# The state's output and the Toeplitz loads issued by GpSimd, an eighth buffer for sample keys and values

## The chip, the cores and the metric

The kernel runs on one core of a Trainium2 chip. The metric is the device time of one execution in microseconds (us). The core's engines run at the same time, each through its own instructions in a fixed order, and wait for each other by semaphores: TensorE (PE in the profile; PEld is its weight load), VectorE (DVE), ScalarE (ACT), GpSimd (POOL) and SyncE (SP), which here does nothing but issue transfers (DMAs). ScalarE issues DMAs too. A DMA that waits for something holds up all that stands behind it in the queue of its issuer.

## What is computed

One inference step of a hybrid decoder layer for a prompt of 1024 tokens and a sample group of 8 x 4 tokens with cached state, all with shared weights. The part that the change touches is the first mixer: attention heads beside a diagonal state-space model (S5), both fed from one projection.

```python
def trunk_layer(x, h0_re, h0_im, mem_k, mem_v, attend, w_in, ...):
    proj = x @ w_in
    q, k, v, u = jnp.split(proj, [D_ATT, 2 * D_ATT, 3 * D_ATT], axis=-1)
    o_att = attend(q, k, v).reshape(Bn, L, D_ATT)
    y_ssm, h_re, h_im = s5_mixer(u, h0_re, h0_im, a_re, a_im, log_dt, b_re, b_im, c_re, c_im, d_skip, w_glu, b_glu)
    mixed = jnp.concatenate([rms_norm(o_att, g_att), rms_norm(y_ssm, g_ssm)], axis=-1) @ w_out
    x = layer_norm(DEEPNORM_ALPHA * x + mixed, ln1_g, ln1_b)
    x = layer_norm(DEEPNORM_ALPHA * x + memory_attention(x, mem_k, mem_v, w_mem_q, w_mem_o), ln2_g, ln2_b)
    ffn = (jax.nn.silu(x @ w_gate) * (x @ w_up)) @ w_down
    return layer_norm(DEEPNORM_ALPHA * x + ffn, ln3_g, ln3_b), k, v, h_re, h_im
```

`s5_mixer` runs, for 32 groups of 16 channels, a complex state of 64 through a scan over the positions, `h_t = A h_(t-1) + B u_t`, with `y_t = Re(C h_t) + D u_t`, then GELU and a gate; it returns the last state as well. For the sample tokens, `attend` reads 1024 cached keys and values.

## The kernel before

Matrix products are made of three float32r products each (high part by high part, high by low, low by high), so a line like L209 to L211 is one step of a product. The run goes through: projection (u, q, k, v) with the state-space model and the sample attention woven in, up to about 345 us; prompt attention, gate and output; memory attention; feed-forward. The change lies in the first of these.

*The state-space model* (`ssm`, L1338 on) runs in two halves (`qf`), 16 of the 32 groups each, stored as 8 pairs of groups. Tokens are cut into chunks of 8. In a half, Bs and CA are built on VectorE and GpSimd (L1426 to L1428), TensorE transposes Bs into ET (L1437) and computes the taps kp (L1448), which go to DRAM as s_kp (L1454). TensorE then makes the chunk inputs from ET and U (L1466), ScalarE puts them into HX (L1468). HX is 128 partitions by 8 pairs by 2 (real, imaginary) by 145 columns. The tile M (named ET in the trace, because it takes over ET's buffer) is the Toeplitz matrix of the taps, read back from s_kp by 8 DMAs (L1471); it needs all L1466 to be over. VectorE then scans HX (`step`, L1479 to L1483): first inside blocks of 8 chunks, then 15 steps over the blocks, the last of which writes column 136. Then HX is corrected (L1495 to L1500), the real part on VectorE and the imaginary on GpSimd, in two blocks of four pairs. TensorE makes the outputs from M and U (L1510) and from CA and HX (L1514), ScalarE applies GELU into Y (L1517, named Bs), which goes out by 8 DMAs (L1522). The state's output (L1519) stores columns 136 to 144 of HX, 9 floats per pair and part.

*The sample attention* (`sample_attn`, `sample_finish`) takes keys (ckT) and values (cv) in chunks of four tiles of 128 x 512, all from one ring of buffers named skv, seven of them; five chunks for each of two groups of sequences. L712 makes the scores from a key tile and the queries qb, which GpSimd lays out (L726) from qs, written by ScalarE in four parts; L772 multiplies a value tile by the probabilities; L778 ends a group; VectorE reads its result in L780.

The order on each engine is set when the program is built, by a scheduler that places all instructions by their dependences; SP's queue holds the skv loads, the DMAs of the state-space model and, later, others.

Of the kernel before, what the change touches and what calls it, by code (L numbers as in the profile page):

```python
# [13 lines left out]
OP = mybir.AluOpType  # L14
# [126 lines left out]
class Body:  # L141
# [145 lines left out]
    def project(self, A, xa, og):  # L287
# [34 lines left out]
        with tc.tile_pool(name="ps_a", bufs=1, space=PSUM) as self.pp2, tc.tile_pool(name="ssm_small", bufs=1) as self.sp, tc.tile_pool(name="ssm_part", bufs=1) as sh, \  # L322
# [47 lines left out]

            ssm = self.ssm()
            next(ssm)

            def between(work, *at):
                for i, _ in enumerate(work):
                    for n, gen in at:
                        if i in n:
                            next(gen, None)

            between(self.gemm(4, 4, xa, evac_q), ((0, 4), ssm))  # L380
            sample = self.sample_attn(sap)
            between(self.gemm(8, 4, xa, evac_k), (range(1, 11), sample), ((5, 10), ssm))
            finish = self.sample_finish(*next(sample))
            between(self.gemm_v(12, 2, lhs_x, [8], evac_v, False), ((0,), finish), ((1,), ssm))
# [311 lines left out]
    def sample_attn(self, ap):  # L696
        nc, a = self.nc, self.a
        v, act, g, mm = nc.vector, nc.scalar, nc.gpsimd, nc.tensor.matmul
        mask, tsel, bsel = (self.t(ap, [128, n], f"sm{n}") for n in (704, 16, 8))
        for d, s in ((mask, a["mask_s"]), (tsel, a["toksel"]), (bsel, a["bsel"])):  # L700
            nc.sync.dma_start(d[:], s)

        def load(src, gr, c):
            t_ = [self.t(ap, [128, 512], "skv", bufs=7) for _ in range(4)]
            for b4 in range(4):
                nc.sync.dma_start(t_[b4][:], a[src][4 * gr + b4, c])
            return t_

        def scores(o, n, q, keys):
            for hp in range(4):  # L710
                for b4 in range(4):
                    mm(o[32 * b4:32 * b4 + 32, :n], q[:, hp, b4].rearrange("p h t -> p (h t)"), keys(b4, hp),  # L712
                       start=hp == 0, stop=hp == 3)

        def masked(gr, j, o, n, s0, m0):
            S, nm = probs[gr][:2]
            v.tensor_tensor_reduce(out=S[:, s0:s0 + n], in0=o, in1=mask[:, m0:m0 + n], scale=-1.0, scalar=3e38,
                                   op0=OP.add, op1=OP.min, accum_out=nm[:, j:j + 1])

        probs = []  # L720
        for gr in range(2):
            qb = self.t(ap, [128, 4, 4, 8, 4], "qb", bufs=2)
            g.memset(qb[:], 0.0)
            for hp in range(4):
                for z in range(2):
                    g.tensor_copy(out=qb[64 * z:64 * z + 64, hp, :, 2 * hp + z, :],  # L726
                                  in_=self.qs[64 * z:64 * z + 64, hp, 16 * gr:16 * gr + 16].rearrange("p (b t) -> p b t", t=4))
            probs.append((self.t(ap, [128, 672], "sS", bufs=2), self.t(ap, [128, 3], "snm", bufs=2), qb))
            for c in range(5):
                if c % 4 == 0:  # L730
                    ps = self.psq()
                kt = load("ckT", gr, c)
                scores(ps[:, 128 * (c % 4):], 128, qb, lambda b4, hp: kt[b4][:, 128 * hp:128 * hp + 128])
                if c >= 3:
                    w = 512 if c == 3 else 128
                    masked(gr, c - 3, ps[:, :w], w, 512 * (c - 3), 512 * (c - 3))
                yield
        yield ap, probs, load, scores, masked, tsel, bsel

    def sample_finish(self, ap, probs, load, scores, masked, tsel, bsel):  # L740
        nc, a = self.nc, self.a
        v, act, g, mm = nc.vector, nc.scalar, nc.gpsimd, nc.tensor.matmul
# [13 lines left out]
        for gr, (S, nm, qb) in enumerate(probs):  # L756
# [12 lines left out]
            for c in range(5):  # L769
# [2 lines left out]
                    mm(po[32 * b4:32 * b4 + 32, :], PT[:, 128 * c + 32 * b4:128 * c + 32 * b4 + 32], vt[b4][:],  # L772
                       start=c == 0, stop=False)
                yield
            vs = self.t(ap, [128, 512], "skv", bufs=7)
            nc.sync.dma_start(vs[:32], self.s_v[1024:1056, :])
            for b4 in range(4):
                mm(po[32 * b4:32 * b4 + 32, :], PT[:32, 640 + 32 * b4:672 + 32 * b4], vs[:32], start=False, stop=True)  # L778
# [556 lines left out]
    def ssm(self):  # L1335
        nc, a, sp, sh = self.nc, self.a, self.sp, self.sh
        H_ = lambda tag, shape: self.t(sh, list(shape), tag)
        v, g, act, mm = nc.vector, nc.gpsimd, nc.scalar, nc.tensor.matmul  # L1338
# [69 lines left out]
        H = lambda tag, shape: self.t(sh, list(shape), tag)  # L1408
        for qf in range(2):
            gs = slice(8 * qf, 8 * qf + 8)  # L1410

            Bs, CA = H("Bs", (128, 8, 2, 8, 16)), H("CA", (128, 8, 2, 9, 16))
            for i in range(4):
                l2, g2 = slice(2 * i, 2 * i + 2), slice(8 * qf + 2 * i, 8 * qf + 2 * i + 2)
                d1, d2, p1, p2 = (H(n_, (128, 2, 9, 16)) for n_ in ("d1", "d2", "p1", "p2"))
# [42 lines left out]
            HX = H("HX", (128, 8, 2, 145))  # L1458
# [9 lines left out]
                act.copy(HX[:, gl, :, 9:145], ps[:, 0:272].rearrange("p (r c) -> p r c", r=2))  # L1468
            M = H("ET", (128, 16, 128))
            for i in range(8):  # L1470
                nc.sync.dma_start(M[16 * i:16 * i + 16], self.s_kp[qf, :, :, 16 * i:16 * i + 128])  # L1471
            X = HX[:, :, :, 9:137].rearrange("p g r (J j) -> p g r J j", j=8)
            qa = lambda e_: e_[:, gs].unsqueeze(2)
            m1, m2 = S("w1", (128, 8, 2, 16)), S("w2", (128, 8, 2, 16))
# [1 line left out]
            def step(dst, src, are, aim, naim, w):  # L1476

                b1 = are.unsqueeze(2).unsqueeze(3).to_broadcast([128, 8, 2, w])
                tt(out=m1[:, :, :, :w], in0=src, in1=b1, op=OP.mult)  # L1479
                tt(out=m2[:, :, 0, :w], in0=src[:, :, 1], in1=naim.unsqueeze(2).to_broadcast([128, 8, w]), op=OP.mult)  # L1480
                tt(out=m2[:, :, 1, :w], in0=src[:, :, 0], in1=aim.unsqueeze(2).to_broadcast([128, 8, w]), op=OP.mult)
                tt(out=dst, in0=dst, in1=m1[:, :, :, :w], op=OP.add)
                tt(out=dst, in0=dst, in1=m2[:, :, :, :w], op=OP.add)  # L1483
# [3 lines left out]
                step(X[:, :, :, :, j], X[:, :, :, :, j - 1], QW[:, 0, 0, gs], QW[:, 0, 1, gs], nq[:, 0, gs], 16)  # L1487
            for J in range(1, 16):
                step(X[:, :, :, J, 7:8], X[:, :, :, J - 1, 7:8], QW[:, 7, 0, gs], QW[:, 7, 1, gs], nq[:, 7, gs], 1)
            for hh in range(2):  # L1490
                l4, g4 = slice(4 * hh, 4 * hh + 4), slice(8 * qf + 4 * hh, 8 * qf + 4 * hh + 4)
                for ri, e in ((0, v), (1, g)):
                    w_ = [H(n_, (128, 4, 15, 7)) for n_ in (("d1", "d2"), ("p1", "p2"))[ri]]
                    for sri, q_ in ((0, QW[:, 0:7, ri]), (1, nq[:, 0:7] if ri == 0 else QW[:, 0:7, 0])):
                        e.tensor_tensor(out=w_[sri][:], in0=X[:, l4, sri, 0:15, 7:8].to_broadcast([128, 4, 15, 7]),  # L1495
                                        in1=q_[:, :, g4].rearrange("p n g -> p g n").unsqueeze(2)
                                        .to_broadcast([128, 4, 15, 7]), op=OP.mult)
                    d_ = X[:, l4, ri, 1:16, 0:7]
                    e.tensor_tensor(out=d_, in0=d_, in1=w_[0][:], op=OP.add)
                    e.tensor_tensor(out=d_, in0=d_, in1=w_[1][:], op=OP.add)  # L1500
# [3 lines left out]
            for g0 in range(0, 8, 3):  # L1504
# [11 lines left out]
                for z in range(2):  # L1516
                    act.activation(Y[:].rearrange("p (g z) c -> p z g c", z=2)[:, z, g0:g0 + cnt, :],  # L1517
                                   pz[z][:, :136 * cnt].rearrange("p (g c) -> p g c", c=136), AF.Gelu_apprx_tanh)
            nc.sync.dma_start(a["st"][:, gs], HX[:, :, :, 136:145])  # L1519
            sy = self.s_y[:].rearrange("(g h) (t c) -> h g t c", h=16, t=8)  # L1520
            for t_ in range(8):
                nc.sync.dma_start(sy[:, 16 * qf:16 * qf + 16, t_, :], Y[16 * t_:16 * t_ + 16])  # L1522
# [16 lines left out]
```

## Time and profile before

| | |
|---|---|
| runs, us | 1713.34 median of 3 (1711.29 to 1715.49) |
| profiled execution, us | 1714.67 |
| its span, us | 1712.9 |
| mean granted clock of TensorE | 0.97 |
| busy, us: PE, PEld, DVE, ACT, POOL | 1606.2, 1465.5, 933.9, 599.2, 545.8 |

A row of a timeline says when an instruction starts, how long it takes, what it writes and reads, and in brackets how long the engine had stood idle and who released it. Several equal instructions are one row with a count; one matmul with float32 operands (L712, L772, L1510, L1514) is two in these rows. The granted clock is a share of full speed: 1.00 is 2.4 GHz, 0.50 is 1.2 GHz.

### The profile page before, as it was taken

The page shows a single profiled execution, that of the slowest core. Times are in us where ns is not written, and L with a number is a line of the kernel's source. Part 1 is how long each engine was busy: PE and PEld are TensorE (multiplying, and loading weights), DVE is VectorE, ACT ScalarE, POOL GpSimd, SP SyncE. Part 2 cuts the span into 40 slices and gives each one's busy share as a digit, 9 for nine tenths or more (in the row PEclk, how much of TensorE's full clock was granted, in tenths as well). Part 3 has the DMA queues.
Part 4 walks back from the last instruction along what each step waited for, and adds up shares of the span by engine and source line. Part 5 has one row for each costly group of instructions (what it writes and reads, how often), then busy time and mean ns, then how long its engine had stood idle before and what let it go on. Part 6 is the DMA issues. An engine that isn't in the chain of part 4 may idle for free.

```text
span 1712.9 us, 27751 instructions
## 1 busy us (share of the span) xinstructions
PE 1606.2 (94%) x10910; PEld 1465.5 (86%) x10910; DVE 933.9 (55%) x1769; ACT 599.2 (35%) x1164; POOL 545.8 (32%) x534
## 2 busy tenths in 40 slices
PE   7996888889999997999899899999999999999996
PEld 6995775566666987997699889999999999999995
DVE  7555456057545787225635885455555545544645
ACT  5220221167435155325513543333333333211212
POOL 3413412023223345002115655444444442000133
PEclk9998999889999998999999999999999999999998
DMA  7546865553231346316550213222222224422301
GB/s 261 138 101 166 223 158 162 126 199 103 95 117 65 127 154 228 125 37 210 191 197 13 91 59 100 75 75 75 75 75 75 75 75 141 141 75 68 114 38 65
DMA packets 105299, 200.71 MB, mean 117 GB/s; under 512 B 14480, under 2 KB 61072, under 8 KB 104400
## 3 DMA queue, kind: packets, MB, share of 16 engines
q1 hardware_dynamic: 81936, 139.68, 26.5%
q10 hardware_dynamic: 23232, 59.26, 10.6%
q8 instruction: 86, 1.41, 0.3%
q14 instruction: 45, 0.37, 0.1%
HBM read 153.85 MB, written 45.04 MB: 116 GB/s over the span
## 4 chain that ended last, share of the span: by engine, by line
PE 74%; DVE 9%; DMA 8%; ACT 3%; issue 2%; POOL 2%; SPq 1%; ACTq 0%; POOLq 0%; DVEq 0%
PE g L1051 16%; PE g L209 12%; PE g L210 12%; PE g L211 12%; PE s L1051 7%; DMA wraw<-in_wst_dram 3%; PE s L594 2%; PE s L596 2%; DVE wlo L191 1%; DMA skv<-in_cv_dram 1%; PE q L772 1%; PE g L618 1%; POOL z L855 1%; DMA hr<-s_h 1%; PE s L1514 1%
## 5 line engine op out<-in xcount | busy, mean ns | idle before, releaser
L209 PE MATMUL g<-a0h,whi 128*128 128x384 f32 (+1 forms) x768 | 253.7, 332 | 10.0 <-ACT whi L190 7.8
L211 PE MATMUL g<-a0h,wlo 128*128 128x384 f32 (+1 forms) x768 | 250.4, 326 | 5.4 <-DVE wlo L191 5.4
L210 PE MATMUL g<-a0l,whi 128*128 128x384 f32 (+1 forms) x768 | 251.2, 327 | 1.0 <-DVE a0l L509 1.0
L210 PE MATMUL g<-a1l,whi 128*128 128x384 f32 (+1 forms) x672 | 218.6, 326 | 4.2 <-DVE a1l L337 1.8
L209 PE MATMUL g<-a1h,whi 128*128 128x384 f32 (+1 forms) x672 | 221.4, 330 | 0.9 <-ACT a1h L335 0.9
L211 PE MATMUL g<-a1h,wlo 128*128 128x384 f32 (+1 forms) x672 | 218.4, 325 | 0.0
L209 PEld LDWEIGHTS g<-a0h,whi 128*128 128x128 f32 x768 | 146.4, 191 | 17.4 <-ACT whi L190 8.0
L211 PEld LDWEIGHTS g<-a0h,wlo 128*128 128x128 f32 x768 | 147.0, 191 | 7.1 <-DVE wlo L191 6.1
L190 ACT CAST whi<-wraw 128x1024 fp32r<-128x1024 f32 x84 | 88.0, 1049 | 179.1 <-PE g L210 103.0
L210 PEld LDWEIGHTS g<-a0l,whi 128*128 128x128 f32 x768 | 146.9, 191 | 2.5 <-DVE a0l L509 1.5
L191 DVE TENSOR_TENSOR wlo<-wraw,whi 128x1024 fp32r<-128x1024 f32 x84 | 118.2, 1410 | 47.4 <-ACT whi L190 47.2
L209 PEld LDWEIGHTS g<-a1h,whi 128*128 128x128 f32 x672 | 128.6, 191 | 5.8 <-issue 2.8
L210 PEld LDWEIGHTS g<-a1l,whi 128*128 128x128 f32 x672 | 128.3, 191 | 5.8 <-DVE a1l L337 2.0
L211 PEld LDWEIGHTS g<-a1h,wlo 128*128 128x128 f32 x672 | 128.3, 191 | 0.6 <-issue 0.4
L1044 DVE TENSOR_TENSOR wlo<-wt,wlo 128x512 fp32r<-128x512 f32 x100 | 91.0, 911 | 26.8 <-ACT wlo L1043 25.1
L1043 ACT CAST wlo<-wt 128x512 fp32r<-128x512 f32 x100 | 62.0, 620 | 111.7 <-PE g L1051 83.8
L800 DVE TENSOR_TENSOR z<-z,g 128x384 f32<-128x384 f32 (+1 forms) x96 | 49.2, 519 | 89.0 <-PE g L211 88.9
L808 POOL TENSOR_TENSOR acc<-z 128x384 f32<-128x384 f32 (+1 forms) x6 | 8.5, 1417 | 187.9 <-DVE z L800 174.1
L606 POOL TENSOR_SCALAR S<-S,rD 128x128 f32<-128x128 f32 (+7 forms) x64 | 38.7, 610 | 84.2 <-DVE rD L605 51.1
L855 POOL TENSOR_SCALAR z<-z,vneg,vecs 128x384 f32<-128x384 f32 (+1 forms) x36 | 49.0, 1375 | 43.9 <-DVE z L851 43.9
L1219 POOL TENSOR_SCALAR S<-S,rD 128x256 f32<-128x256 f32 x32 | 15.3, 482 | 113.2 <-DVE rD L1208 105.6
L1041 POOL TENSOR_TENSOR wt<-wraw,wraw 128x512 f32<-128x512 f32 x30 | 39.4, 1313 | 22.0 <-DVE wlo L1044 22.0
(457 smaller groups left out, 4018.8 us busy)
## 6 DMA issues: line engine op xcount, KB each, us to landing
wraw<-in_wst_dram ACTq DMA_DIRECT2D x88, 512.0 KB, 4.0
skv<-in_ckT_dram SPq DMA_DIRECT2D x40, 256.0 KB, 4.9
skv<-in_cv_dram SPq DMA_DIRECT2D x40, 256.0 KB, 3.9
wraw<-in_wst_dram SPq DMA_DIRECT2D x20, 512.0 KB, 4.3
wru<-in_wst_dram SPq DMA_DIRECT2D x20, 512.0 KB, 4.2
hr<-s_h SPq DMA_DIRECT2D x22, 384.0 KB, 3.4
kvm<-in_cmk_dram SPq DMA_DIRECT2D x16, 512.0 KB, 5.0
wraw<-in_cmv_dram SPq DMA_DIRECT2D x16, 512.0 KB, 4.8
```

The source lines that it names most:

```text
L190: self.nc.scalar.copy(h[:], r[:])
L191: self.nc.vector.tensor_tensor(out=l[:], in0=r[:], in1=h[:], op=OP.subtract)
L209: mm(out, wh, xh, start=start, stop=False)
L210: mm(out, wh, xl, start=False, stop=False)
L211: mm(out, wl, xh, start=False, stop=stop)
L606: g.tensor_scalar(out=S[:, :w], in0=S[:, :w], scalar1=rD[:], scalar2=1.0, op0=OP.mult, op1=OP.mult)
L800: self.nc.vector.tensor_tensor(out=z[:, k], in0=z[:, k], in1=ps[:, :n], op=OP.add)
L855: g.tensor_scalar(out=z[:, k], in0=z[:, k], scalar1=sc, scalar2=bi, op0=OP.mult, op1=OP.add)
L1041: g.tensor_tensor(out=src, in0=q[p_], in1=q[q_], op=op)
L1043: act.copy(t_[:, 0], src)
L1044: v.tensor_tensor(out=t_[:, 1], in0=src, in1=t_[:, 0], op=OP.subtract)
L1051: nc.tensor.matmul(ps[:, :n], p_, q_, start=first and k + j == 0, stop=k == 3 and j == 2, skip_group_check=not first)
```

## The change

Three things: the state's output and the eight Toeplitz loads of each half are issued by GpSimd (`g`) instead of SP; the ring of skv gets an eighth buffer; and the correction of HX runs in four blocks of two pairs instead of two of four, so its temporaries (d1, d2, p1, p2) are half as long.

```diff
@@ sample_attn, load @@
-            t_ = [self.t(ap, [128, 512], "skv", bufs=7) for _ in range(4)]
+            t_ = [self.t(ap, [128, 512], "skv", bufs=8) for _ in range(4)]
...
@@ ssm @@
             M = H("ET", (128, 16, 128))
             for i in range(8):
-                nc.sync.dma_start(M[16 * i:16 * i + 16], self.s_kp[qf, :, :, 16 * i:16 * i + 128])
+                g.dma_start(M[16 * i:16 * i + 16], self.s_kp[qf, :, :, 16 * i:16 * i + 128])
...
-            for hh in range(2):
-                l4, g4 = slice(4 * hh, 4 * hh + 4), slice(8 * qf + 4 * hh, 8 * qf + 4 * hh + 4)
+            for hh in range(4):
+                l4, g4 = slice(2 * hh, 2 * hh + 2), slice(8 * qf + 2 * hh, 8 * qf + 2 * hh + 2)
                 for ri, e in ((0, v), (1, g)):
-                    w_ = [H(n_, (128, 4, 15, 7)) for n_ in (("d1", "d2"), ("p1", "p2"))[ri]]
+                    w_ = [H(n_, (128, 2, 15, 7)) for n_ in (("d1", "d2"), ("p1", "p2"))[ri]]
...
-            nc.sync.dma_start(a["st"][:, gs], HX[:, :, :, 136:145])
+            g.dma_start(a["st"][:, gs], HX[:, :, :, 136:145])
```

The load of the sample's own values (L776) takes its buffer from the same ring and gets the 8 as well.

What this does to the order, first on SP in the first half, between the taps (s_kp) and the second chunk of keys. Before:

```order
L1454 DMA s_kp<-Bs_857 64x1x240 x4
L1471 DMA ET_1061<-s_kp 16x16x128 x8
L706 DMA skv_1568<-in_ckT_dram 128x512
L706 DMA skv_1618<-in_ckT_dram 128x512
L706 DMA skv_1619<-in_ckT_dram 128x512
L706 DMA skv_1620<-in_ckT_dram 128x512
L1519 DMA out_dram<-HX_1010 128x16x9
L706 DMA skv_1621<-in_ckT_dram 128x512
```

And now:

```order
L1454 DMA s_kp<-Bs_857 64x1x240 x4
L706 DMA skv_1642<-in_ckT_dram 128x512
L706 DMA skv_1643<-in_ckT_dram 128x512
L706 DMA skv_1644<-in_ckT_dram 128x512
L706 DMA skv_1645<-in_ckT_dram 128x512
L706 DMA skv_1695<-in_ckT_dram 128x512
```

Both transfers of the state-space model are gone from between the keys; the first key here is now the ninth of all, before it was the eighth.

On GpSimd in the second half, where HX is corrected (p are its temporaries, qw the powers of A; qb here is a small sum of the sample attention). Before:

```order
L790 TENSOR_TENSOR qb_2897<-qb_2897 128x32
L791 TENSOR_TENSOR qsum_133<-qb_2897 128x16
L1495 TENSOR_TENSOR p_334_2590<-HX_2407,qw_651 128x420
L1495 TENSOR_TENSOR p_335_2591<-HX_2407,qw_651 128x420
L1499 TENSOR_TENSOR HX_2407<-HX_2407,p_334_2590 128x4x15x7
L1500 TENSOR_TENSOR HX_2407<-HX_2407,p_335_2591 128x4x15x7
```

And now:

```order
L1471 DMA ET_2482<-s_kp 16x16x128 x8
L790 TENSOR_TENSOR qb_2945<-qb_2945 128x32
L791 TENSOR_TENSOR qsum_133<-qb_2945 128x16
L1495 TENSOR_TENSOR p_342_2614<-HX_2431,qw_651 128x210
L1495 TENSOR_TENSOR p_343_2615<-HX_2431,qw_651 128x210
L1499 TENSOR_TENSOR HX_2431<-HX_2431,p_342_2614 128x2x15x7
L1500 TENSOR_TENSOR HX_2431<-HX_2431,p_343_2615 128x2x15x7
L1495 TENSOR_TENSOR p_346_2626<-HX_2431,qw_651 128x210
L1519 DMA out_dram<-HX_2431 128x16x9
L1495 TENSOR_TENSOR p_347_2627<-HX_2431,qw_651 128x210
L1499 TENSOR_TENSOR HX_2431<-HX_2431,p_346_2626 128x2x15x7
L1500 TENSOR_TENSOR HX_2431<-HX_2431,p_347_2627 128x2x15x7
```

The Toeplitz loads stand ahead of these operations, and the state's output stands inside the second block of the correction, behind its first operation; what is left of this block and the two blocks after it come behind the output. In the first half the loads stand ahead of the qb copies (L726), and the output stands between the third and the fourth operation of the first block.

## Rows read from the trace of the kernel before

**Rows 1.** Page, part 4: the chain that ended last, share by engine.

```profile
PE 74%; DVE 9%; DMA 8%; ACT 3%; issue 2%; POOL 2%; SPq 1%; ACTq 0%; POOLq 0%; DVEq 0%
```

**Rows 2.** Timeline of PE: start, length, instruction, count [wait before it <- releaser].

```profile
127.55 1.08 PE L712 MATMUL q<-skv,qb 128*32 128x128 f32 x32
...
134.56 1.06 PE L712 MATMUL q<-skv,qb 128*32 128x128 f32 x26
...
154.84 1.92 PE L712 MATMUL q<-skv,qb 128*32 128x128 f32 x26 [13.41 <-DMA skv<-in_ckT_dram]
...
167.06 0.73 PE L1510 MATMUL s<-U,ET 128*128 128x136 f32 x4
...
210.16 0.41 PE L712 MATMUL q<-skv,qb 128*32 128x128 f32 x2 [2.41 <-DMA skv<-in_ckT_dram]
...
254.73 1.04 PE L772 MATMUL q<-skv,qb 128*32 128x512 f32 x2 [3.54 <-DMA skv<-in_cv_dram]
...
278.40 1.06 PE L778 MATMUL q<-skv,qb 32*32 32x512 f32 x8
...
295.15 0.50 PE L1514 MATMUL s<-HX,CA 64*128 64x136 f32 x4 [2.77 <-DVE HX L1500]
...
305.27 1.91 PE L772 MATMUL q<-skv,qb 128*32 128x512 f32 x2 [8.19 <-DMA skv<-in_cv_dram]
```

**Rows 3.** Windows: stretch, length, busy PE, PEld, DVE, ACT, POOL, clock, DMA share, GB/s.

```profile
155.00:160.50 5.50, 5.50 (x39) 5.00 (x35) 0.00 (x0) 0.00 (x0) 0.00 (x0) 0.52 0.72 194
...
255.00:260.00 5.00, 5.00 (x17) 2.61 (x16) 4.83 (x12) 0.00 (x0) 0.00 (x0) 0.66 0.94 350
...
305.20:313.00 7.80, 7.73 (x16) 2.50 (x16) 0.00 (x0) 0.00 (x0) 0.00 (x0) 0.50 0.74 263
```

**Rows 4.** Timeline of SP's queue: start, time to issue, transfer, count.

```profile
103.20 5.18 SPq L1471 DMA_DIRECT2D ET<-s_kp  x8
...
128.64 2.39 SPq L706 DMA_DIRECT2D skv<-in_ckT_dram  x4
...
142.72 0.39 SPq L1519 DMA_DIRECT2D out_dram<-HX  x1
...
143.21 40.15 SPq L706 DMA_DIRECT2D skv<-in_ckT_dram  x20
...
242.34 5.79 SPq L1471 DMA_DIRECT2D ET<-s_kp  x8
```

**Rows 5.** Line L1519: SP's waits, min/median/max ns, first and last start.

```profile
L1519 SPq EVENT_SEMAPHORE  x2: 8522/11098/13674, 134.2 to 279.9; - x2
```

**Rows 6.** DMA issues: count, KB each, median us to landing; last row 140 to 160 us.

```profile
skv<-in_ckT_dram SPq DMA_DIRECT2D x40, 256.0 KB, 4.9
...
ET<-s_kp SPq DMA_DIRECT2D x16, 128.0 KB, 6.0
...
out_dram<-HX SPq DMA_DIRECT2D x2, 72.0 KB, 11.4
...
skv<-in_ckT_dram SPq DMA_DIRECT2D x8, 256.0 KB, 11.2
```

**Rows 7.** Timeline of POOL; then tile HX: count, min/median/max ns.

```profile
111.07 1.62 POOL L726 COPY qb<-qs 64x16 f32<-64x16 f32 x4 [36.47 <-ACT qs L298]
...
124.94 2.24 POOL L726 COPY qb<-qs 64x16 f32<-64x16 f32 x4 [1.03 <-ACT qs L298]
...
L1495 POOL TENSOR_TENSOR p<-HX,qw x8: 1189/1394/1989, 136.4 to 293.5; 128x420 f32<-128x420 f32 x8
```

**Rows 8.** Timeline of DVE.

```profile
141.67 0.98 DVE L1483 TENSOR_TENSOR HX<-HX,w 128x16 f32<-128x16 f32 x1
...
218.40 0.45 DVE L1428 TENSOR_TENSOR CA<-d,d 128x288 f32<-128x288 f32 x1
...
279.60 0.69 DVE L780 TENSOR_TENSOR sS<-q,sm 128x512 f32<-128x512 f32 x1 [12.79 <-PE q L778]
...
292.36 1.17 DVE L1483 TENSOR_TENSOR HX<-HX,w 128x16 f32<-128x16 f32 x1
```

More of the change, by code (lines that the diff above doesn't have):

```diff
@@ L774, in sample_finish @@
                 yield
-            vs = self.t(ap, [128, 512], "skv", bufs=7)
+            vs = self.t(ap, [128, 512], "skv", bufs=8)
             nc.sync.dma_start(vs[:32], self.s_v[1024:1056, :])
@@ L1489, in ssm @@
                 step(X[:, :, :, J, 7:8], X[:, :, :, J - 1, 7:8], QW[:, 7, 0, gs], QW[:, 7, 1, gs], nq[:, 7, gs], 1)
-            for hh in range(2):
-                l4, g4 = slice(4 * hh, 4 * hh + 4), slice(8 * qf + 4 * hh, 8 * qf + 4 * hh + 4)
+            for hh in range(4):
+                l4, g4 = slice(2 * hh, 2 * hh + 2), slice(8 * qf + 2 * hh, 8 * qf + 2 * hh + 2)
                 for ri, e in ((0, v), (1, g)):
-                    w_ = [H(n_, (128, 4, 15, 7)) for n_ in (("d1", "d2"), ("p1", "p2"))[ri]]
+                    w_ = [H(n_, (128, 2, 15, 7)) for n_ in (("d1", "d2"), ("p1", "p2"))[ri]]
                     for sri, q_ in ((0, QW[:, 0:7, ri]), (1, nq[:, 0:7] if ri == 0 else QW[:, 0:7, 0])):
-                        e.tensor_tensor(out=w_[sri][:], in0=X[:, l4, sri, 0:15, 7:8].to_broadcast([128, 4, 15, 7]),
+                        e.tensor_tensor(out=w_[sri][:], in0=X[:, l4, sri, 0:15, 7:8].to_broadcast([128, 2, 15, 7]),
                                         in1=q_[:, :, g4].rearrange("p n g -> p g n").unsqueeze(2)
-                                        .to_broadcast([128, 4, 15, 7]), op=OP.mult)
+                                        .to_broadcast([128, 2, 15, 7]), op=OP.mult)
                     d_ = X[:, l4, ri, 1:16, 0:7]
```

## The prediction, made before the changed kernel was run

> **What bounds the kernel now.** Read the chain that ended last first: TensorE holds 74% of it, VectorE 9%, DMA 8% [rows 1]. So a saving counts only where TensorE stands still, and TensorE's own timeline is the next view. In the stage that the change touches, from 125 to 345 us, it waits five times for longer than 2 us [rows 2]: 13.41 us ending at 154.84, 2.41 at 210.16, 3.54 at 254.73, 2.77 at 295.15, 8.19 at 305.27. Four are for sample keys or values (skv), one for HX on VectorE. The windows after the long ones show a second cost: TensorE runs at a granted clock of 0.52, 0.66 and 0.50 of full [rows 3], that is wholly or partly at 1.2 instead of 2.4 GHz, after having stood still.
>
> Why the skv come late is read from SP, the engine that issues them. SP takes its queue in order. The state's output (L1519) sits in it and needs the last scan step on VectorE (L1483). SP stands at that wait twice, 8.5 us from 134.2 and 13.7 us from 279.9 [rows 4, 5], and no skv behind it is issued. Then there is a second effect: the output moves as 128 x 16 pieces of 9 floats, 72 KB in 2,048 pieces, and takes 11.4 us to land, and eight skv loads issued behind it took 11.2 us at the median, against 4.9 for all [rows 6]. 143.21 (first load behind it) to 154.84 (its matmul) is that 11.6 us. The wait at 254.73 has another issuer: the Toeplitz loads (L1471) got out at 242.34 only, since they need TensorE to finish reading the tile they overwrite, and the next values were queued behind them [rows 4].
>
> **The change part by part.** The sum is made against the profiled execution, 1714.67 us (span 1712.9 and 1.8 around it); the median of the runs is 1713.34, 1.3 below.
>
> *A, the wait at 154.84.* In the new order SP holds nothing but skv loads there. The load in question needed only the chunk before it: SP has issued its predecessors by 131.0 [rows 4], so from 135.6, when TensorE frees that buffer [rows 2], plus 4.9 us it would land at 140.5, before the 141.4 at which TensorE stopped. With eight buffers a whole second chunk of four is loaded ahead, and it is not even that close. Gain 13.4. The half-clock stretch behind it is 5.5 us at 0.52; at full clock it needs 52% of that: 2.6. A = -16.0.
>
> *B, the wait at 210.16.* 2.41 us, but TensorE's next step needs Bs and CA of the second half, which VectorE finishes at 218.85 [rows 8]; that chain starts when the first half's result is stored and so moves with A, no further. Between 0 and 2.4; I take -1.0.
>
> *C, the wait at 254.73.* With the Toeplitz loads gone from SP the values are issued as their buffers come free. 3.54, and 5 us at 0.66 give 1.7: -5.2. Is this passed on? VectorE's scan has step L780 in its row, which waited 12.79 us for TensorE's L778 [rows 8]; all scan steps behind it start earlier when TensorE does. Up to 12.8 us are, so all of C.
>
> *D, the waits at 295.15 and 305.27.* The second goes with the output: 8.19, and 7.8 us at 0.50 give 3.9, together -12.1. The first wait is replaced by new ones. Count from the end of L778 (279.46). TensorE has 12.9 us of its own work until L1514. VectorE ends the scan (L1483) at 293.53, 14.1 us after [rows 8]; L1500 behind it takes some 0.6, so the first block of two pairs is ready at 14.7 and TensorE waits 1.8. The second block's imaginary part is corrected on GpSimd, where now the output's issue stands among its operations and waits for that same L1483; then comes the issue itself, g, then three operations of half the old width. The old ones took 1.2 to 2.0 us [rows 7]; half is about 0.7, 2.1 for three. With g = 3 the block is ready at 14.1 + 3 + 2.1 = 19.2; TensorE has some 2.9 us of matmuls in between (an estimate: four L1510 at 0.73 for two [rows 2], as long again for the L1514, two L772), comes at 17.6 and waits 1.6. New waits 3.4 against 2.77: +0.6. A wait of this size was followed by 1.7 us lost to the clock in C; +1.5 here. And skv loads now fly beside the output, not behind it: between 0 and 6.3 us later (11.2 less 4.9 [rows 6]); nearest is the low end, since most are issued before the output, +2. D = -12.1 + 0.6 + 1.5 + 2 = -8.0.
>
> *The price of g.* No transfer is issued by GpSimd in the trace before. From below: SP's issue of the same output, 0.39 us [rows 4]. From above: the output's own way to land, 11.4 us [rows 6]. I take 3, nearer to the issue row, since issuing is what the engine does. The Trainium skill (DMA: Bandwidth & Descriptors, section "SWDGE vs HWDGE vs iDMA") says that for GpSimd's transfers a program on its cores writes the descriptors; its section "Latency and other measured facts" gives about 1 us to the first byte instead of 0.6, by which the sum would be some 3 us lower; no run here shows either yet.
>
> *The first half's output on GpSimd.* It stands inside the correction of HX there. The scan ends at 142.65 [rows 8]; issue, then 13 operations of 0.7 bring the last block to 151.8 + g. Without A's stall TensorE comes to L1510 at 167.06 - 16 = 151 [rows 2] and to the last block some 9 us later. So g up to about 8 is covered: 0. If this cover is gone, each further us costs one.
>
> *The Toeplitz loads on GpSimd.* Eight issues of 256 pieces each, 2,048 pieces again, from 103.2 on, when TensorE has read the tile [rows 4]. Behind them stand the qb copies, the last of which ends at 127.18, right before the first L712 at 127.55 [rows 2, 7]. These come in four bursts, tied to ScalarE, the first at 111.07 of 1.6 us, the last at 124.94 of 2.2, some 8 us in all; the loads may hold GpSimd until about 119, 16 us, 2 us each, before TensorE feels it. SP's issue was 0.72 each (5.79 for eight [rows 4]), the landing 6.0 [rows 6]. I take 1.2 each: 0. In the second half GpSimd has nothing to do in that time.
>
> *The finer correction.* Four blocks of two pairs instead of two of four: the same elements in twice the operations on VectorE and GpSimd, 8 more on each per half, some 0.1 to 0.2 us each; it lies beside TensorE's work except for the operations counted above: 0. The smaller w tiles only make room for the buffer.
>
> **Sum:** -16.0 - 1.0 - 5.2 - 8.0 = -30.2; 1714.7 - 30.2 = 1684.5. I give 1684. Everything after 370 us follows unchanged and starts earlier; the stage from 345 to 365 has waits of its own, which move along.
>
> **The rivals.**
>
> *GpSimd's issuing is slow (ends slower).* For: the work is 2,048 pieces for each output and for each set of Toeplitz loads; if it goes piece by piece, one price G holds for all three. Then TensorE waits G - 16 for qb, G - 8 for the first HX and G - 3 beyond the forecast in the second. At G = 12 that is 4 + 9 = 13: 1698. It eats the 30.2 when 3G - 27 = 30.2, G = 19; from 19.5 us on (9.5 ns a piece) the kernel is slower, at 25 us by 18: 1733. Against: the output lands in 11.4 us altogether when SP issues it, so G over 11 would need the issue to be slower than the transfer.
>
> *The transfers still collide.* Eight skv loads behind the output were slow since it had the DMA engines [rows 6]. If it does the same from another queue, D loses the 4.3 us left up to 6.3, and the clock stays low some 3 us longer: 1692. The Trainium skill (DMA: Bandwidth & Descriptors, section "Issuing engines are not separate DMA queues") speaks for it: transfers of all issuers run on the same 16 engines and interleave, and issuing from several saves the issuer's time alone. By that rule the 11.2 us would remain for whatever is in flight; but A's gain comes from SP's wait being gone, which the rule leaves.
>
> *It doesn't do what it says.* SP keeps other waits among the skv: U for the second half (L1433) and the kernel taps (L1454), which need TensorE and VectorE. If C's wait only moves to L1454, or the scan doesn't follow TensorE, C and B are lost: 1691. Without any effect but g the time is that of before.
>
> **How the numbers follow.** Forecast 1679 to 1690: 0.48. Better, with B whole and no new waits in D (1674 to 1679): 0.06. Collision or C lost, 1690 to 1700: 0.20. Slow issue in part, G of 10 to 16, 1692 to 1706: 0.08. The gain eaten to within 0.3% of before, which is about what a measurement of this kernel can tell from no change (5 us): 0.07. Slower: 0.11. So faster 0.82, same 0.07, slower 0.11. The range from 1674 to 1706 leaves out 0.18 above and little below.
>
> **What would show it.** A: no wait at TensorE's L712 after 135 us, and L1510 near 151. C: the wait for L778 on VectorE's L780 shrinks to about 8 us. D: TensorE's wait before L1514 is named by GpSimd and some 2 to 4 us long. g: the gap on GpSimd between the operations around L1519; over 8 us there, or qb copies that end after 128, is the slow rival. The forecast is wrong at its root if SP still stands between skv loads for more than some 5 us with TensorE idle.

## The result, and the profile after

The changed kernel takes 1688.01 us (median of 4 runs, 1687.41 to 1694.87), the kernel before 1714.41 (4 runs, 1711.29 to 1715.54): ratio 0.9858, 95% interval 0.9829 to 0.9887. That is 26 us less by the medians and 24 by the ratio, where 30 were forecast. The profiled execution is the slowest of the four, 1694.87 us with a span of 1693.1. A second set of runs of the same kernel (label e10 below) gave 1689.90 and a profiled execution of 1689.09; where the two traces differ, both numbers are given.

The chain that ended last holds more of TensorE and less of VectorE, of the DMAs and of ScalarE than before [rows 1] (page, part 4):

```profile
PE 79%; DMA 7%; DVE 6%; issue 2%; ACT 2%; POOL 2%; SPq 1%; POOLq 0%; ACTq 0%; DVEq 0%
```

The waits of TensorE over 1.5 us from 125 to 300 us (timeline of PE; in brackets the wait and its releaser), to be laid beside [rows 2]:

```profile
152.39 1.92 PE L712 MATMUL q<-skv,qb 128*32 128x128 f32 x26 [4.08 <-DMA skv<-in_ckT_dram]
...
206.09 1.69 PE L1437 MATMUL s<-ident,Bs 128*128 128x128 f32 x5 [4.40 <-ACT ET L1439]
...
247.80 1.05 PE L772 MATMUL q<-skv,qb 128*32 128x512 f32 x2 [1.90 <-DMA skv<-in_cv_dram]
...
293.17 1.04 PE L772 MATMUL q<-skv,qb 128*32 128x512 f32 x2 [2.86 <-DMA skv<-in_cv_dram]
```

Of the five waits three remain, all shorter: 13.41 has become 4.08, 3.54 has become 1.90, 8.19 has become 2.86. The one before L1514 and that of 2.41 are gone. L1437 waits 4.40 for ET, where it waited 3.72 before:

```profile
214.62 1.12 PE L1437 MATMUL s<-ident,Bs 128*128 128x128 f32 x4 [3.72 <-ACT ET L1439]
```

This line is from the kernel before; [rows 2] and the prediction's count of five leave it out. The windows behind the waits (columns as in [rows 3]) show that the clock still falls around the first, to 0.50, which is 1.2 GHz. First the kernel before, then two windows of the changed one:

```profile
146.60:160.20 13.60, 5.36 (x37) 4.86 (x38) 4.29 (x5) 0.00 (x0) 3.96 (x4) 0.50 0.70 128
...
152.40:164.40 12.00, 12.00 (x71) 10.00 (x72) 0.46 (x3) 2.19 (x3) 0.00 (x0) 0.50 0.53 192
206.00:212.00 6.00, 5.78 (x25) 5.39 (x26) 4.75 (x10) 2.98 (x7) 2.23 (x4) 0.50 0.89 300
```

Before, most of the half clock lay in the long wait, where it costs nothing: TensorE worked in 5.36 of the 13.60 us. Now it works in all of the 12.00 us.

SP now issues loads only where before it stood at the output's wait [rows 4, 5] (timeline of SP's queue):

```profile
127.40 28.27 SPq L706 DMA_DIRECT2D skv<-in_ckT_dram  x20
...
253.37 34.57 SPq L706 DMA_DIRECT2D skv<-in_cv_dram  x20
```

On GpSimd (timeline of POOL) the eight Toeplitz issues take 4.66 us together, the output's issue 1.22 and 1.21, and the last qb copy ends at 125.95, so no later than before [rows 7]:

```profile
102.58 4.66 POOL L1471 DMA_DIRECT2D ET<-s_kp  x8 [29.24 <-ACT HX L1468]
...
123.66 2.29 POOL L726 COPY qb<-qs 64x16 f32<-64x16 f32 x4 [1.01 <-ACT qs L298]
...
138.47 1.22 POOL L1519 DMA_DIRECT2D out_dram<-HX  x1 [0.63 <-DVE HX L1483]
...
278.33 1.21 POOL L1519 DMA_DIRECT2D out_dram<-HX  x1 [0.33 <-DVE HX L1500]
```

Why the keys are still late stands in the DMA view, beside [rows 6]. From 137 to 156 us, GB/s in 40 slices of 0.475 us; then the issues there, and the keys alone as issued from 138 to 142 us, the last of these four by itself (issued at 139.61), and from 142 to 148 us (count, KB each, median us to landing):

```profile
GB/s 229 293 229 261 247 130 181 368 366 405 397 337 159 65 43 13 9 4 13 39 73 99 105 70 129 78 71 79 146 227 182 167 189 371 408 360 388 390 393 352
...
out_dram<-HX POOLq DMA_DIRECT2D x1, 72.0 KB, 13.7
...
skv<-in_ckT_dram SPq DMA_DIRECT2D x4, 256.0 KB, 4.0
...
skv<-in_ckT_dram SPq DMA_DIRECT2D x1, 256.0 KB, 12.7
...
skv<-in_ckT_dram SPq DMA_DIRECT2D x4, 256.0 KB, 10.8
```

The output takes 13.7 us to land, and during it what the core's DMA engines move falls from some 400 to 4 GB/s and stays under 130 from 143 to 150 us. The key issued at 139.61, the twentieth, takes 12.7 us, and it is the one that TensorE waits for until 152.39; the four behind it take 10.8, as the four issued right behind the output did before (10.9 to 12.3; the 11.2 of [rows 6] counts later, faster ones in). So the wait that is left is not for the key of the old wait: that was the twelfth, which now lands at 135.08, 2 us before TensorE uses it.

For the experiments one table carries most. It gives the start of five steps of TensorE, which every kernel here runs, in each profiled execution: the first L712, the scores on the sample's own keys (L712 on ks), the first and the last start of L778, and the last L594, in the last part of prompt attention. "Median" is the time of all runs, "ratio" that to the kernel before as measured beside it, with its 95% interval. The parts that differ lie ahead of the last L594, and yet the traces take from 457.8 to 463.3 us from there to the first L1051 of the feed-forward; so a single execution is read by the marks and not by its end. The marks scatter too. The first L712 already starts 1.2 and 3.7 us earlier in the two traces of the changed kernel than before, and so does the first L1437 (66.9 and 64.1 against 68.2), which runs ahead of both transfers; two traces of one kernel differ as much there (e4 64.3, e11 67.0). So what the change does is read from the first L712 on.

| kernel | first L712 | ks scores | first L778 | last L778 | last L594 | median, us | ratio |
|---|---|---|---|---|---|---|---|
| before | 127.5 | 225.4 | 278.4 | 328.1 | 550.5 | 1710.7 to 1714.4 | 1 |
| changed | 126.3 | 216.3 | 265.7 | 304.8 | 530.7 | 1688.0 | 0.9858 (0.9829 to 0.9887) |
| changed, second set (e10) | 123.8 | 214.1 | 265.0 | 304.9 | 527.5 | 1689.9 | 0.9865 (0.9848 to 0.9882) |
| e1, output back on SP | 125.1 | 212.6 | 264.4 | 308.5 | 532.6 | 1696.6 | 0.9896 (0.9861 to 0.9930) |
| e2, Toeplitz loads back on SP | 126.2 | 212.0 | 264.0 | 304.8 | 528.8 | 1694.9 | 0.9894 (0.9862 to 0.9926) |
| e3, seven buffers | 125.3 | 216.9 | 267.9 | 306.5 | 532.8 | 1693.9 | 0.9884 (0.9854 to 0.9913) |
| e5, before, output on GpSimd | 125.2 | 214.4 | 267.9 | 310.0 | 532.8 | 1699.5 | 0.9926 (0.9902 to 0.9950) |
| e6, before, Toeplitz on GpSimd | 126.5 | 223.9 | 275.8 | 323.8 | 549.6 | 1710.6 | 0.9990 (0.9976 to 1.0005) |
| e9, before, four blocks | 125.2 | 221.7 | 274.8 | 321.7 | 547.6 | 1712.3 | 0.9989 (0.9978 to 1.0000) |
| e7, before, four blocks, eight buffers | 125.1 | 209.6 | 261.2 | 304.6 | 529.0 | 1695.4 | 0.9903 (0.9876 to 0.9930) |
| e8, changed, output twice | 125.3 | 217.0 | 267.5 | 313.5 | 540.0 | 1699.6 | 0.9923 (0.9893 to 0.9954) |
| e4, changed, output packed | 124.0 | 204.1 | 255.4 | 290.7 | 517.7 | 1685.7 | 0.9827 (0.9798 to 0.9856) |
| e11, the same again | 126.4 | 205.5 | 257.2 | 292.5 | 518.9 | 1682.8 | 0.9818 (0.9802 to 0.9834) |
| e12, packed, all issued by SP | 125.2 | 205.8 | 257.7 | 291.2 | 516.3 | 1682.1 | 0.9812 (0.9794 to 0.9830) |

### The profile page after: what moved, and what is told of

Same layout as the page of the kernel before. It is cut to its first block, busy times and chain, and to the rows that moved or that the text cites. A ratio compares the mean times of both kernels' runs of the same rounds, so it can differ in the third digit from the quotient of the medians.

```text
span 1693.1 us, 27820 instructions
## 1 busy us (share of the span) xinstructions
PE 1607.1 (95%) x10910; PEld 1468.4 (87%) x10910; DVE 932.8 (55%) x1785; ACT 598.8 (35%) x1164; POOL 558.6 (33%) x568
## 2 busy tenths in 40 slices
DMA packets 97683, 200.71 MB, mean 119 GB/s; under 512 B 10384, under 2 KB 52880, under 8 KB 96784
## 3 DMA queue, kind: packets, MB, share of 16 engines
q10 hardware_dynamic: 23232, 59.26, 10.8%
q0 software_dynamic: 864, 2.25, 0.9%
## 4 chain that ended last, share of the span: by engine, by line
PE 79%; DMA 7%; DVE 6%; issue 2%; ACT 2%; POOL 2%; SPq 1%; POOLq 0%; ACTq 0%; DVEq 0%
PE g L1051 16%; PE g L209 13%; PE g L211 13%; PE g L210 13%; PE s L1051 7%; PE s L594 2%; PE s L596 2%; DMA skv<-in_cv_dram 1%; DMA wraw<-in_wst_dram 1%; PE g L618 1%; DMA skv<-in_ckT_dram 1%; POOL z L855 1%; DVE wlo L191 1%; PE q L772 1%; DMA hr<-s_h 1%
## 5 line engine op out<-in xcount | busy, mean ns | idle before, releaser
L209 PE MATMUL g<-a0h,whi 128*128 128x384 f32 (+1 forms) x768 | 255.4, 334 | 12.6 <-ACT whi L190 9.4
L209 PEld LDWEIGHTS g<-a0h,whi 128*128 128x128 f32 x768 | 147.9, 193 | 19.8 <-ACT whi L190 9.6
L209 PEld LDWEIGHTS g<-a1h,whi 128*128 128x128 f32 x672 | 127.5, 190 | 5.7 <-issue 2.8
L1219 POOL TENSOR_SCALAR S<-S,rD 128x256 f32<-128x256 f32 x32 | 15.2, 478 | 113.3 <-DVE rD L1208 105.7
L594 PE MATMUL s<-K,Q 64*128 64x256 f32 (+1 forms) x128 | 42.2, 438 | 5.1 <-DVE nm L602 5.1
```

The source lines that it names most:

```text
L209: mm(out, wh, xh, start=start, stop=False)
L594: mm(ps[:, 32 * nf:w], q, k[:, 128 * max(qt - 1, 0):128 * qt + 128], start=True, stop=True)
```

## The experiments

### One part undone

**The output back on SP.** In the changed kernel:

```diff
-            g.dma_start(a["st"][:, gs], HX[:, :, :, 136:145])
+            nc.sync.dma_start(a["st"][:, gs], HX[:, :, :, 136:145])
```

> The changed kernel with one part undone: the state's output is issued by SP again, the Toeplitz loads stay on GpSimd, eight buffers. Theory 1, the prediction's: what cost time was SP standing at the output's wait, with loads behind it. Then A and D come back: some 13 us of waits in the first half, 8 in the second, with their half clock about 20 to 25 us over the changed kernel, 1708 to 1713. Theory 2: the issuer matters little once the ring has eight buffers, because the order on SP now has two whole chunks of keys ahead of the output, SP reaches it only at about 137 us, when the scan is nearly over, and the keys behind it were late in the changed kernel too. Then the first half stays as it is, only the second half's output stands before values, and the time is 0 to 8 us over the changed kernel, 1688 to 1696.

Measured: 1696.6 us, just over the upper end of theory 2 (1696). TensorE's waits before keys and values, and SP's issues around the first output:

```profile
149.46 0.63 PE L712 MATMUL q<-skv,qb 128*32 128x128 f32 x2 [2.77 <-DMA skv<-in_ckT_dram]
...
288.57 1.92 PE L772 MATMUL q<-skv,qb 128*32 128x512 f32 x2 [8.61 <-DMA skv<-in_cv_dram]
```

```profile
137.43 0.39 SPq L1519 DMA_DIRECT2D out_dram<-HX  x1
137.92 19.14 SPq L706 DMA_DIRECT2D skv<-in_ckT_dram  x12
```

SP's waits at the output (count, min/median/max ns, first and last start):

```profile
L1519 SPq EVENT_SEMAPHORE  x2: 2537/5597/8657, 134.9 to 268.0; - x2
```

In the first half the 13.41 of [rows 2] do not come back: the wait is 2.77, shorter than with GpSimd as issuer, and SP stands 2.5 us at the output instead of 8.5 [rows 5]. In the second half SP stands 8.7 us and the wait of 8.61 is back. So with 36-byte pieces D goes with the issuer, and A does not go with it alone.

**The Toeplitz loads back on SP.**

```diff
-                g.dma_start(M[16 * i:16 * i + 16], self.s_kp[qf, :, :, 16 * i:16 * i + 128])
+                nc.sync.dma_start(M[16 * i:16 * i + 16], self.s_kp[qf, :, :, 16 * i:16 * i + 128])
```

> The changed kernel with one part undone: the Toeplitz loads are issued by SP again, output on GpSimd, eight buffers. Theory 1, the prediction's: C (3.5 us of wait for values and 1.7 of clock) comes back, +5, 1693. Theory 2: with eight buffers two whole chunks of values are on the chip before SP stands at the Toeplitz loads, and TensorE doesn't notice: 0, 1688.

Measured: 1694.9, by the median theory 1's. The wait of C is 3.58 us instead of 1.90, but from the first L778 to the last L594 the marks stand within 2 us of the two traces of the changed kernel, and the intervals of the ratios overlap. The wait of C does follow the issuer in every trace: with the Toeplitz loads on GpSimd it is 1.35 to 2.18 us (eight traces), with them on SP 3.20 to 3.82 (six). What this is worth in time beside the other parts stays open between 0 and 7 us.

**Seven buffers.** `bufs=8` to `bufs=7` in both places, the rest as changed.

> The changed kernel with one part undone: seven buffers for keys and values again, both transfers on GpSimd, correction in four blocks. Theory 1, the prediction's: the buffer adds little where SP doesn't stand still, 0 to 4 us, 1688 to 1692. Theory 2: it is the buffer that carries the gain of A, since without it the fourth tile of the second chunk and all behind it are issued one chunk of TensorE's work later and fall beside the state's output, which takes 14 us to land: +8 to +15, 1696 to 1703.

Measured: 1693.9, between the two. The first wait is 5.73 us against 4.08, more small waits for keys follow (0.94, 1.09, 2.62 before 202 us), and the marks are 0.6 to 5.3 us later. With GpSimd issuing, the buffer is worth about 4 us, with an interval that reaches 0.

### One part alone

**The output on GpSimd alone** (the diff's last line in the kernel before):

> The kernel before with one part of the change alone: the state's output issued by GpSimd; Toeplitz loads on SP, seven buffers, correction in two blocks. Theory 1, the prediction's: A and D are this part's, 16 + 8 less than before, 1690. Theory 2, from the three kernels with one part undone, each of which lost only 6 to 9 us: the parts stand in for each other. With seven buffers the keys are still issued beside the output and wait as in the kernel with seven buffers (5.7 us in the first half, 2.2 in the second), and C stays: 13.4 - 5.7, 8.2 - 2.2 and the half clock of both, some 18 to 20 less than before, 1694 to 1697.

Measured: 1699.5 us, 11 less than before, short of both theories. The first wait falls to 3.31, the last to 2.17; C's stays at 3.46. Beside it, **the Toeplitz loads on GpSimd alone** (the `L1471` line of the diff):

> The kernel before with one part of the change alone: the Toeplitz loads issued by GpSimd; output on SP, seven buffers. Theory 1, the prediction's: C only, 5 less, 1709. Theory 2: SP reaches the output's wait as before, so A and D stay whole (13.4 and 8.2 us of wait); C's 3.5 is covered in part by a new one: 0 to 3 less, 1711 to 1714.

Measured: 1710.6 beside 1710.7, ratio 0.9990 with 1 inside the interval; the waits of A and D are only 1.3 and 1.1 us shorter, nearly as theory 2 has it:

```profile
152.43 1.92 PE L712 MATMUL q<-skv,qb 128*32 128x128 f32 x26 [12.09 <-DMA skv<-in_ckT_dram]
...
301.03 1.91 PE L772 MATMUL q<-skv,qb 128*32 128x512 f32 x2 [7.10 <-DMA skv<-in_cv_dram]
```

**Eight buffers and four blocks, both transfers on SP** (the diff without its two `dma_start` lines):

> The kernel before with one part of the change alone: eight buffers, and the correction in four blocks that makes room for them; both transfers on SP. Theory 1, the prediction's: SP's standing is the cause, the buffer gives 2 to 4 at most, 1710 to 1712. Theory 2: A is the buffer's as much as the issuer's. With the eighth buffer the whole second chunk of keys stands before the output, SP comes to it at about 137 instead of 134 with four more tiles on the chip, and the first wait falls to some 3 us as where the output alone was put back on SP; D (8.6 there) and C stay. 13.4 - 3 and some 2 of half clock, 10 to 14 less than before, 1700 to 1704.

Measured: 1695.4 us, 15 less, more than either theory gave. To split it, **the four blocks alone**, with seven buffers:

> The kernel before with one part of the change alone: the correction of HX in four blocks of two pairs instead of two of four; both transfers on SP, seven buffers (eight don't fit without the shorter temporaries). Theory 1, the prediction's: the finer correction costs and gains nothing, 1711 as before. Theory 2: VectorE does the first block of the correction in among the last scan steps, and half as long a block lets the last step (L1483, which frees the state's output) end earlier, at 137.3 us in the kernel with eight buffers and four blocks against 142.6 before; SP then stands 4 to 5 us less in each half, the waits of 13.4 and 8.2 us shrink by as much, with some of the half clock behind them: 8 to 12 less, 1699 to 1703.

Measured: 1712.3 against 1714.0, in time theory 1. VectorE does end the last scan step earlier, and SP stands 5.0 and 10.3 us instead of 8.5 and 13.7 [rows 5], as theory 2 said; but the waits hardly shrink. The two kernels beside each other, first e9, then e7, TensorE and SP:

```profile
150.51 1.92 PE L712 MATMUL q<-skv,qb 128*32 128x128 f32 x26 [11.35 <-DMA skv<-in_ckT_dram]
...
298.34 1.91 PE L772 MATMUL q<-skv,qb 128*32 128x512 f32 x2 [8.18 <-DMA skv<-in_cv_dram]
```

```profile
126.34 2.49 SPq L706 DMA_DIRECT2D skv<-in_ckT_dram  x4
137.61 0.39 SPq L1519 DMA_DIRECT2D out_dram<-HX  x1
138.09 24.88 SPq L706 DMA_DIRECT2D skv<-in_ckT_dram  x12
```

```profile
147.99 0.41 PE L712 MATMUL q<-skv,qb 128*32 128x128 f32 x2 [1.23 <-DMA skv<-in_ckT_dram]
149.72 0.63 PE L712 MATMUL q<-skv,qb 128*32 128x128 f32 x2 [1.32 <-DMA skv<-in_ckT_dram]
...
284.29 1.06 PE L772 MATMUL q<-skv,qb 128*32 128x512 f32 x1 [7.46 <-DMA skv<-in_cv_dram]
```

```profile
126.20 8.67 SPq L706 DMA_DIRECT2D skv<-in_ckT_dram  x8
137.42 0.40 SPq L1519 DMA_DIRECT2D out_dram<-HX  x1
137.92 17.49 SPq L706 DMA_DIRECT2D skv<-in_ckT_dram  x12
```

Same issuer, same correction, the output issued at the same moment (137.6 and 137.4), and the first wait is 11.35 with seven buffers and 2.55 with eight. What differs is SP's order: with seven, 11 keys are issued ahead of the output, with eight 16. That is A's wait, and it goes without GpSimd.

The four parts do not add: 12.7 (e5), 1.7 (e6) and 16.6 (e7, with the blocks' 1.9 in it), each worked out from its ratio, make 31 apart and 23 to 24 together. The output's issue and the buffer remove the same wait, A's.

### The pieces

**The output packed.** In the changed kernel, with a new tile of 128 x 144:

```diff
-            g.dma_start(a["st"][:, gs], HX[:, :, :, 136:145])
+            so = H("so", (128, 8, 2, 9))
+            g.tensor_copy(out=so[:], in_=HX[:, :, :, 136:145])
+            g.dma_start(a["st"][:, gs], so[:])
```

> The changed kernel, and GpSimd first copies columns 136 to 144 of HX into a tile of 128 x 144, so that the output leaves as 128 runs of 576 bytes instead of 2,048 of 36. Theory 1: the 36-byte pieces hold the DMA engines. In the changed kernel the moved bytes fall to 4 to 40 GB/s from 143 to 149 us, while the output is on its way, and keys issued behind it take 10.8 us instead of 4 to 5. Packed, the output lands in 3 to 6 us, the waits of 4.08 us before L712 and of 2.86 before L772 go, with the half clock behind them (7.6 us at 0.50 and 3 at 0.69: 3.8 and 0.9): 11.6 less, 1676 to 1680. Theory 2: the waits are those of the ring (a tile is loaded only when an older one is read), and the output's size and shape don't matter: no change, 1687 to 1690, with the copy's time on GpSimd as a loss of at most 1.

Measured: 1685.7 us, between the two theories. Both waits are gone, as theory 1 has it, and prompt attention ends 10 to 13 us earlier than in the changed kernel; the median is only 2 to 4 us lower, so it was run again beside the changed kernel:

> The changed kernel as it is, as the measure for the two packed ones beside it on the same chip: 1686 to 1692 by its own result; nothing is told apart by it alone.

> The changed kernel with the output packed by GpSimd, once more, beside the changed kernel. Theory 1: the gain seen in the traces of the stage (prompt attention begins 15 us earlier than in the changed kernel) reaches the end but for the 2 us given back at its head and some clock: 6 to 12 less than the changed kernel. Theory 2: what is gained in this stage is given back where the weights and attention limit the run: the same within 0.3%, 0 to 4 less, as the two medians so far (1685.7 and 1688.0) would have it.

Measured: 1689.9 and 1682.8, 7.1 less, theory 1. The GB/s from 137 to 156 us and the landing of the output, then the windows where TensorE stood still or ran at half clock in the changed kernel:

```profile
GB/s 336 375 272 243 295 96 219 378 393 412 388 405 438 37 86 320 94 190 352 291 107 199 331 397 285 250 332 243 51 194 287 263 408 401 393 388 138 103 22 0
...
out_dram<-so POOLq DMA_DIRECT2D x1, 72.0 KB, 3.6
```

```profile
149.00:153.00 4.00, 4.00 (x41) 3.21 (x37) 2.38 (x7) 1.28 (x1) 2.32 (x4) 1.00 0.84 265
153.00:157.00 4.00, 4.00 (x25) 4.00 (x24) 0.00 (x0) 0.91 (x2) 0.00 (x0) 1.00 0.36 139
```

The same 72 KB in 128 runs of 576 bytes land in 3.6 us instead of 13.7, the rate no longer falls to a few GB/s for microseconds, TensorE is busy throughout and the clock stays at 1.00. The Trainium skill (DMA: Bandwidth & Descriptors, section "Rules for kernel authors") says that a non-contiguous last dimension becomes one descriptor per element and should be rearranged; no run here has that case, since the last dimension of this store is contiguous and only short, nine floats. What the short pieces cost, this pair of runs shows.

**The output twice.** The changed kernel with a second issue into a scratch tensor:

```diff
             g.dma_start(a["st"][:, gs], HX[:, :, :, 136:145])
+            g.dma_start(self.s_st[:, gs], HX[:, :, :, 136:145])
```

> The changed kernel, and GpSimd issues the state's output a second time, into a scratch tensor, right behind the first. Theory 1: the 2,048 pieces of 36 bytes hold the DMA engines for as long as they last, so twice as many hold them twice as long: the waits of 4.1 us before L712 and 2.9 before L772 grow by 8 to 12 each, half clock behind them, 1708 to 1720; GpSimd's second issue adds 1.2 each. Theory 2: keys and values are late from the ring, not from the output: only the 1.2 us on GpSimd, covered in the first half, 1688 to 1691.

Measured: 1699.6 us, 10 to 12 over the changed kernel, against 0 to 3 by theory 2. The mechanism is theory 1's, its price is not. All line numbers here are one higher:

```profile
153.89 1.91 PE L713 MATMUL q<-skv,qb 128*32 128x128 f32 x26 [6.58 <-DMA skv<-in_ckT_dram]
...
293.00 1.68 PE L773 MATMUL q<-skv,qb 128*32 128x512 f32 x2 [4.57 <-DMA skv<-in_cv_dram]
```

The waits grow by 2.5 and 1.7 us and two new ones of 1.5 and 1.1 follow; the second copy lands in 20.3 us at the median and the first in 15.2, 5 and 8 us behind the first, so in part side by side, and the marks lose most, 6 to 7 us, between the first and the last L778.

**Packed, and both transfers on SP.** The kernel before with eight buffers, four blocks and the packed output, issued by SP:

> The kernel before with eight buffers, four blocks and the packed output (GpSimd copies, as in the packed kernel), but both transfers issued by SP as before. Theory 1, the prediction's: SP standing at the output's wait is what costs; in the second half it stands some 8 us there as with the buffer alone, and TensorE waits 5 to 8 us for values, the clock falls behind it, and the Toeplitz loads cost C: 10 to 15 more than the packed kernel with GpSimd as issuer. Theory 2: with eight buffers it is the 36-byte pieces that make keys and values late; packed, what stands behind the output lands in 4 to 5 us and the order holds it early enough: 0 to 4 more than the packed kernel.

Measured: 1682.1 us beside 1682.8: theory 2. In the first half this kernel differs from e7 in the packing alone (GpSimd's copy and the pieces): SP has the same order, and issues the output at the same time.

```profile
137.53 0.34 SPq L1521 DMA_DIRECT2D out_dram<-so  x1
137.98 25.08 SPq L706 DMA_DIRECT2D skv<-in_ckT_dram  x16
```

The two waits of e7, 2.55 us together, are gone. In the second half the order changed as well (the scheduler puts the output behind 16 values of the second group instead of 8, and SP does not stand at it), so what the pieces and the place do there isn't told apart. Against the changed kernel measured beside it e12 is 7.8 us less, and it and e11 are the fastest of all. Packing alone, in the kernel before with seven buffers, was not run, so what it brings by itself stays open.

## Why the prediction came out as it did

The time fell where it was forecast, within the likeliest case's range (1679 to 1690), but as a sum of terms that missed in both directions, so the closeness is in part luck; and the reason given for the largest term was only half of it. By the marks, changed kernel against before (first trace, second trace):

| step | predicted | measured |
|---|---|---|
| up to the first L712 | 0 | -1.2, -3.7 |
| A and B, from there to the ks scores | -17.0 | -7.9, -7.6 |
| C, from there to the first L778 | -5.2 | -3.6, -2.1 |
| D, first to last L778 | -8.0 | -10.6, -9.8 |
| last L778 to last L594 ("follows unchanged") | 0 | +3.5, +0.2 |
| sum | -30.2 | -19.8, -23.0 |

The first and the last of these steps as windows (columns as in [rows 3]), before and then changed, first trace:

```profile
127.55:225.40 97.85, 76.66 (x761) 66.27 (x761) 48.85 (x118) 15.34 (x32) 34.63 (x35) 0.90 0.72 194
...
328.10:550.50 222.40, 213.20 (x1626) 151.69 (x1619) 119.69 (x352) 111.10 (x288) 59.18 (x105) 0.96 0.37 119
```

```profile
126.31:216.30 89.99, 79.41 (x761) 69.03 (x760) 47.97 (x126) 15.44 (x32) 35.67 (x44) 0.89 0.83 221
...
304.80:530.70 225.90, 216.73 (x1629) 154.85 (x1622) 119.45 (x352) 111.20 (x289) 58.93 (x105) 0.95 0.36 118
```

- **A** is the term that failed, in its wait and in its clock. The load that it follows, the twelfth key, did come in time, as it said. But it follows that one load alone, and takes every later key to land 4.9 us after its issue; the twentieth, issued 1.1 us behind the output, took 12.7, and a wait of 4.08 stays. The prediction charged the collision in D (+2) and forgot it in A, where keys are issued beside the output just as values are. The clock was to give 2.6 back. Instead the half clock costs more than before, an estimate of 6.0 us (half of the 12.00 that TensorE works at 0.50) against 2.7 (half of 5.36): the idle time of the step fell by 10.6 us, from 21.2 to 10.6, and the same 761 matmuls were busy 2.8 us longer. The 4.08 and the 6.0 together are 10.1 of the 16.0. The rival of the colliding transfers was right on the mechanism and placed it in the wrong half too. The Trainium skill's rule named there (DMA: Bandwidth & Descriptors, section "Issuing engines are not separate DMA queues") agrees with the 12.7 and the 10.8 us; what it leaves out, the loads that no longer stand behind SP's wait, is the gain that e5 shows.
- **A's cause** was told as SP's standing, with the buffer as a bonus ("it is not even that close"). e5 and e7 show two changes that each suffice: the output on GpSimd alone takes the wait from 13.41 to 3.31, the buffer (with the four blocks, which alone leave 11.35) to 2.55. In the first half the buffer without GpSimd is even ahead of the whole change (from the first L712 to the ks scores 84.5 us against 90.0 and 90.3).
- **B**: the chain of Bs and ET limits this place, as forecast: L1437 waits 4.40, where it waited 3.72 before; the keys' 2.41 is split, in the first trace, into several under 0.8. All waits before L712 and L1437 from 188 us on come to 6.4 us instead of 7.8.
- **C**: the wait went from 3.54 to 1.90 instead of to nothing, and the clock behind it stayed at 1.00 in one trace, 0.71 in the other. VectorE's wait for L778 in L780 shrank from 12.79 to 9.98 (11.63 in the second trace) where 8 was named. e6 shows that alone this part is worth between 4 us less and 1 more (its interval); e5 and e7, where the Toeplitz loads stay on SP, still have a wait of 3.46 and 3.20 there.
- **D** came out 1.8 to 2.6 better, since the new waits of 3.4 us before L1514 didn't come: g is 1.2 and not 3, nearer the lower bound of 0.39. In the place of these waits stands one of 2.86 for a value that flew beside the output, which answers to the +2, with some half clock behind it, which answers to the 1.5.
- **g and the Toeplitz loads**: 1.22 for the output's issue, 0.58 for each Toeplitz issue against 1.2 assumed; the qb copies end at 125.95, and the correction on GpSimd at 150.1, before TensorE's first L1510 at 154.23 (151.76 in the second trace; about 151 was named). The rival of slow issuing is out.
- **The finer correction** at 0: right in time (e9: 1.7 less, interval to 0), wrong in reason. It lets VectorE end the scan about 5 us earlier, and this didn't pay since what is late is the output's way to DRAM with the keys beside it.
- **Behind the stage** the forecast had everything follow unchanged. In all other kernels here 0.2 to 4.6 us are lost again between the last L778 and the last L594. In the changed kernel it is not waiting: TensorE is idle for 9.2 us in this step before and 9.2 after (8.3 in the second trace), and busy for 213.2 before and 216.7 after (214.3), with three matmuls more. At the granted clocks of 0.96 and 0.95 that is longer time at half clock. Why the clock falls for longer there, no run shows.

## What to carry to other kernels

A load that is late behind another DMA can be late because its issuer stood still, because its buffer came free late, or because the other DMA holds the engines: the trace shows the first as an event wait in the issuer's queue and the last as a landing time of its own, and each has another cure. Look at the shape of the transfer before moving it to another queue: here, with eight buffers, a copy of 0.4 to 1.6 us into a contiguous tile left the same time with either issuer (1682.8 and 1682.1 us). Undo each part as well as doing it alone, since two parts that remove the same wait each look like the cause. And when a late load is mended, look at the next ones: which of them are now issued beside the transfer that made the first one late.

## What the runs showed of the hardware

- A store of 128 x 16 pieces of 36 bytes (72 KB), issued once, took 10.1 to 12.7 us to land when SP issued it and 11.3 to 17.5 from GpSimd; as 128 runs of 576 bytes 2.9 to 5.3 from either. The 256 KB loads that SP issued while the small pieces were under way took 8.4 to 12.9 us at the median of each store; those around the packed store took 2.5 to 6.0. Whether it is the number of the pieces, their 36 bytes or that they are stored and not loaded, no run tells apart.
- GpSimd's issue of 2,048 pieces took 1.21 to 1.36 us, of 256 pieces 0.56 at the median, of 128 runs 0.62; SP's issue of the same took 0.39 to 0.40, 0.61 at the median and 0.34 to 0.38. It is not a price per piece on either.
- Half clock costs only where TensorE works: the 26 matmul records of L712 behind the first wait take 1.92 us at 0.50, where the same 26 take 1.06 at full clock [rows 2]; of 13.60 us at 0.50 before, 8.24 lay in a wait.
- The pieces that GpSimd issues do not appear one by one in the count of packets: the page's queue of software DMAs holds 864 packets for 2.25 MB, that is for two outputs and sixteen Toeplitz loads of together 8,192 pieces, and the packets under 512 B fall from 14,480 to 10,384, by the two outputs' 4,096.

```profile
q0 software_dynamic: 864, 2.25, 0.9%
```

So a count of packets does not show what small pieces cost when GpSimd issues them; the landing time does.
